# Plain products' results added by accumulating transfers, and dense matmuls dealt by engine time, in a transformer-layer kernel on one core

## The chip, the cores and the metric

The kernel runs on one core of a Trainium2 chip. Its engines are TensorE (PE: matmuls, with PEld for the loading of weights), VectorE (DVE), ScalarE (ACT), GpSimd (POOL) and SyncE (SP), which issues most of the transfers. Each engine works through its own queue in order; engines wait for one another by semaphores. Data lies in device memory (DRAM), in the on-chip memory (SBUF, 128 partitions) and in the matmul accumulators (PSUM).

The metric is the device time of one execution in microseconds (us); the median of several runs counts. A profiled execution also has a span, from its first to its last instruction.

## The reference

One layer, 2048 tokens, width 1024. The mixer has eight heads of stick-breaking attention (strictly causal) and eight heads of softmax attention over chunks with a relative bias; the MLP is a squared ReLU with 4096 hidden columns. Everything is float32.

```
mod = silu(c) @ w_ada + b_ada                 # shifts, scales and gates
h = rmsnorm(x, g_norm1) * (1 + sc1) + sh1
q_sb, k_sb, v_sb, q_ca, k_ca, v_ca = split(h @ w_in)
o_sb = stick_breaking_attention(q_sb, k_sb, v_sb)
o_ca = chunked_relpos_attention(rmsnorm(q_ca, g_q), rmsnorm(k_ca, g_k), v_ca, rel_bias)
x = x + gt1 * (concat(o_sb, o_ca) @ w_o)
h = rmsnorm(x, g_norm2) * (1 + sc2) + sh2
x = x + gt2 * (square(relu(h @ w1)) @ w2)     # the output
```

## The kernel before

All matmuls are done on pairs: a float32 operand is split by `split` (line 139) into a high part (a cast on ScalarE) and the remainder (a subtraction on VectorE), and `mm3` (line 206) multiplies them in three matmuls. The tokens stand in four blocks of 512 columns (`TB`); a block is `2 * mb + odd`, with `mb` the half of the sequence and `odd` the block in it. The residual stream lies in DRAM as `scr_x[block, row]`, eight rows of 128 channels; row `HK * r + n` is written as `r` (upper or lower half of the channels) and `n` (0 to 3).

**Projections** come first (to about 410 us), and then **attention** (to about 1277 us). Attention is a list of units: a head, a group `g` of 512 queries and, for stick-breaking, a block `c` of keys. Each unit takes four steps (`STEPS`), one for each 128 queries. The loop at line 1234 does for step i, in this order: the transposes of the weights of step i - 8 (`LAG`), the scan or softmax of step i (`soft1`: a sigmoid on ScalarE and a scan on VectorE into "p"), the split of the transposed weights ("wth", "wtl"), the matmuls with the values ("acc"), the scores of step i + 1 ("z", "cz", "ct"), and then `fill`. `fill` (line 1164) puts dense matmuls into TensorE's queue: the projections of the other two blocks ("pf") and the output projection ("po"), 1152 of them in all, taken from a list of generators. How many it takes follows from a credit: a share of the step is divided by the shares still to come and multiplied by the matmuls still to come. Before, the share is a constant of the unit: 0.7 for a stick-breaking unit on the diagonal, 1.0 off it, 0.9 for a softmax unit (0.68 in the last group), 0.6 in the eight closing steps. After each row block of results the dealing rests for a step, and for four at the start of some pieces; at changes between the kinds of units 4 or 8 matmuls are added.

**The MLP** (from line 1282) multiplies block matrices by a scheme of seven products in place of eight (Strassen's, in Winograd's form), and within most products once more: `First` makes the hidden rows, seven products per pair of row blocks, first for `mb` 1 and then for `mb` 0. Of the seven products of the second matrix, 1 and 6 are done plainly (`Second`, 16 steps of 12 matmuls) and the other five, `DOUBLE`, are themselves done in seven (`Outer`, 56 steps of 6 matmuls; the loop at line 1927). The products of both halves are joined in the doubled ones, and both halves have plain ones of their own. The steps form one list; `at(n, job)` hangs a job on step n, `later.add(k, job)` on the k-th tick from now, and `prepare` splits operands ahead of their step into a pool of eight tiles.

The plain products leave "s": product 1's result is needed by block (r 0, odd 1), and the sum of 1 and 6 by (0, 0), (1, 1) and (1, 0). `update` (line 1647) adds them to the residual stream, per half 16 times: SP loads the row from `scr_x` into a tile ("xu" in the second half's hidden products, two buffers lent by pool `rp`; else "txu", out of seven of pool `tp`), `weigh` (one VectorE instruction) adds "s" times the gate, and three ticks later SP stores the row. For `mb` 1 these updates stand in plain product 6 and in the following hidden products of `mb` 0 (four rows in each 16 steps); for `mb` 0 they stand in plain product 6, and in products 2, 3 and 4, where those of product 4 write the output.

Doubled product i loads the residual rows that it adds to (`load_x`, "txo" and "cxo"), adds its own results to them and stores them in `scr_x` or, where they are done, in the output. Products 7 and 5 serve two blocks each and have 16 such adds, the others 8. `half_sum` (line 1802) makes the sums of hidden rows ("r"), four VectorE instructions of 1024 columns for each kind; product 5 needs one kind more. `plan` places the loads and sums of the next product.

Of the kernel before, what the change touches and what calls it, by code (L numbers as in the profile page):

```python
# [79 lines left out]
def encoder_kernel(ctx, tc, xT, c, g1, g2, w_in, w_rest, gqk, bias, w_o, w1, w2, w_ada, b_ada, out):  # L80
# [5 lines left out]
    WIN, NEAR = 640, 384  # L86
    cpool = ctx.enter_context(tc.tile_pool(name="cpool", bufs=1))
# [90 lines left out]
    def norm_diagonal(pl, y, tg):  # L178
        dg = pl.tile([P, 4, P], F32, tag="ndg", name=f"ndg{tg}", bufs=1)
# [5 lines left out]
    def norm_rstd(pl, pp, acc, tg, meanwhile=None):  # L185
        y = norm_powers(pl, norm_columns(pp, acc, tg), tg)
        if meanwhile:
            meanwhile()
        return norm_diagonal(pl, y, tg)
# [488 lines left out]
    if True:  # L678
# [426 lines left out]
        def finish_row(g, n, ps, xr):  # L1105
# [28 lines left out]
            def spread(y):  # L1134
                dg = norm_diagonal(op, y, f"m{g}")
# [98 lines left out]
        for i in range(len(steps) + LAG):  # L1234
# [32 lines left out]
            fill(front.weight if front else 0.6, turns.get(i, 0))  # L1267
# [17 lines left out]
    DOUBLE = (7, 5, 2, 3, 4)  # L1285
# [10 lines left out]
    if True:  # L1296
# [43 lines left out]
        def norm2(tb, step):  # L1340
# [14 lines left out]
            def second():  # L1355
                dg = norm_rstd(np2, fresh, acc, f"m{tb}")
# [99 lines left out]
        class First(Step):  # L1456
# [29 lines left out]
            def fetch(self, m=None):  # L1486
                d = self.load()
                for n in range(4) if m is None else (m,):
# [3 lines left out]
                    elif pr == 5 and not self.mb:  # L1492
                        t = np2.tile([P, 4, P], F32, tag="ndg", name=f"s{self.nm}_{pr}", bufs=1).rearrange("p a b -> p (a b)")
# [227 lines left out]
        class Outer(Step):  # L1721
# [62 lines left out]
            def load_x(self, b):  # L1784
                home = kept if self.i in (5, 7) and b in ("22", "11") else temp
                for n in range(2):
                    Outer.outs[b, n] = []
                    for r, odd in {2: ((0, 1),), 3: ((0, 0),), 4: ((1, 1),), 7: ((1, 1), (1, 0)), 5: ((0, 0), (1, 0))}[self.i]:
# [3 lines left out]
                        Outer.outs[b, n].append((x, mb, row, odd, self.i in (2, 3, 4) or (self.i == 5 and mb and r)))  # L1792
# [81 lines left out]
        for mb in (1, 0):  # L1874
# [22 lines left out]
            if mb:  # L1897
# [29 lines left out]
        for i in DOUBLE:  # L1927
# [123 lines left out]
```

## Time and profile before

| | us |
|---|---|
| median of three runs | 2542.36 (2541.83 to 2547.02) |
| the profiled execution, whole | 2545.14 |
| the profiled execution, span | 2543.4 |
| granted TensorE clock, mean | 0.999 |

Columns of the views: a group of instructions has its line (a helper's, L42, for nearly all), engine, operation, "out<-in" by the names of the tiles, shape and count, then busy time in us, the mean of one in ns, the idle time of the engine before them and what ended it. Matmuls overlap: the next starts before the last has ended, and the ends are modelled, so that a short wait of TensorE doesn't show as idle. A row of a timeline has start, length, engine and tiles, with the idle time before it in brackets; SPq rows are transfers at their issue.

### The profile page before, as it was taken

The numbers are of one execution on the slowest core, as the hardware profiler recorded it, in microseconds if no ns is written. First come the engines' busy times: TensorE is split into PE (matmuls) and PEld (weight loads), VectorE is DVE, ScalarE is ACT, GpSimd is POOL, SyncE is SP. The second block draws the span as 40 slices with busy tenths as digits, with TensorE's granted clock in tenths as the row PEclk, the third lists the DMA queues.
The fourth block names the chain that finished last, engine by engine and source line by source line (L and its number), as shares of the span: only waits on it lengthen the run. The fifth ranks groups of instructions, "written<-read, shape, count | busy, mean of one in ns | idle before, by whom it ended". The sixth has DMA issues, their size and how long they took to land.

```text
span 2543.4 us, 39545 instructions
## 1 busy us (share of the span) xinstructions
PE 2513.3 (99%) x12388; PEld 2095.6 (82%) x12388; DVE 2053.9 (81%) x3609; ACT 1510.3 (59%) x2893; POOL 746.0 (29%) x1128
## 2 busy tenths in 40 slices
PE   9999999999999999999999999999999999999999
PEld 7888888888888888887988888888878888888887
DVE  7656767887789878999768777779877759899998
ACT  6333425668866677666755555566545546566665
POOL 4330154777776667776620000000000000000000
PEclk9999999999999999999999999999999999999999
DMA  9879969789977788866787889995998996868884
GB/s 362 323 296 365 351 267 301 208 243 287 290 234 237 236 250 274 265 212 206 218 310 254 302 279 318 329 362 195 328 331 283 313 365 261 329 241 308 282 300 124
DMA packets 305361, 714.66 MB, mean 281 GB/s; under 512 B 32768, under 2 KB 92160, under 8 KB 293504
## 3 DMA queue, kind: packets, MB, share of 16 engines
q1 hardware_dynamic: 303856, 707.43, 81.2%
q10 hardware_dynamic: 1296, 4.72, 0.5%
q8 instruction: 98, 1.61, 0.3%
q14 instruction: 111, 0.91, 0.1%
HBM read 485.00 MB, written 227.02 MB: 280 GB/s over the span
## 4 chain that ended last, share of the span: by engine, by line
PE 80%; DVE 10%; ACT 4%; issue 3%; DMA 3%; POOL 1%; SPq 0%; DVEq 0%; POOLq 0%; ACTq 0%
PE ps L42 24%; PE ps_s L42 14%; PE pt L42 11%; PE acc L42 6%; PE wt L42 6%; PE pf L42 4%; PE z L42 4%; PE po L42 4%; PE pq L42 3%; DVE opr L42 2%; DVE p L42 2%; PE cz L42 1%; DVE ol L42 1%; PE ct L42 1%; DVE r L42 1%
## 5 line engine op out<-in xcount | busy, mean ns | idle before, releaser
L42 PE MATMUL ps<-h,opw 128*128 128x512 f32 x1512 | 358.6, 389 | 0.0
L42 ACT CAST wth<-wt 128x512 fp32r<-128x512 f32 (+3 forms) x544 | 257.0, 483 | 166.7 <-PE wt L42 157.5
L42 POOL TENSOR_TENSOR b<-p 128x512 f32<-128x512 f32 (+1 forms) x320 | 292.0, 912 | 168.7 <-DVE p L42 93.8
L42 DVE TENSOR_TENSOR wtl<-wt,wth 128x512 fp32r<-128x512 f32 (+3 forms) x544 | 291.0, 546 | 57.6 <-ACT wth L42 55.6
L42 PEld LDWEIGHTS ps<-h,opw 128*128 128x128 f32 x1512 | 283.7, 188 | 58.9
L42 PE MATMUL pt<-w,ht 128*128 128x512 f32 x1248 | 288.2, 391 | 0.0
L42 PE MATMUL ps_s<-h,opw 128*128 128x512 f32 x1152 | 279.4, 392 | 4.0 <-DVE cp L42 3.4
L42 PEld LDWEIGHTS pt<-w,ht 128*128 128x128 f32 x1248 | 233.0, 188 | 47.7
L42 DVE TENSOR_TENSOR_SCAN p<-z,p,zero 128x512 f32<-128x512 f32 x192 | 245.7, 1281 | 25.6 <-ACT z L42 18.1
L42 PEld LDWEIGHTS ps_s<-h,opw 128*128 128x128 f32 x1152 | 216.8, 189 | 51.1 <-DVE cp L42 4.7
L42 ACT CAST opr<-r 128x512 fp32r<-128x512 f32 x280 | 174.4, 624 | 134.5 <-PE ps L42 75.9
L42 PE MATMUL ps<-opr,ol 128*128 128x512 f32 x960 | 222.2, 390 | 0.7 <-DVE opr L42 0.6
L42 PE MATMUL acc<-wth,v 128*128 128x512 f32 (+3 forms) x544 | 220.6, 410 | 0.0
L42 PEld LDWEIGHTS ps<-opr,ol 128*128 128x128 f32 x960 | 179.6, 188 | 40.9 <-DVE opr L42 3.5
L42 ACT ACTIVATE z<-z 128x512 f32<-128x512 f32 (+1 forms) x320 | 166.5, 521 | 55.4 <-PE z L42 49.4
L42 DVE TENSOR_TENSOR opr<-r,opr 128x512 fp32r<-128x512 f32 x280 | 184.9, 687 | 10.7 <-ACT opr L42 9.9
L42 PE MATMUL z<-k,q 128*128 128x512 f32 (+3 forms) x640 | 185.7, 372 | 7.7 <-DVE p L42 7.0
L42 PE MATMUL acc<-wtl,v 128*128 128x512 f32 (+3 forms) x544 | 185.4, 347 | 0.0
L42 PE MATMUL ps<-oph,opv 128*128 128x512 f32 x768 | 176.0, 390 | 0.8 <-DVE oph L42 0.3
L42 PE MATMUL wt<-ident,b 128*128 128x128 f32 x1088 | 171.3, 273 | 0.9 <-DVE p L42 0.6
L42 PEld LDWEIGHTS ps<-oph,opv 128*128 128x128 f32 x768 | 143.9, 188 | 32.4 <-DVE oph L42 1.2
L42 PEld LDWEIGHTS wt<-ident,b 128*128 128x128 f32 x1088 | 136.4, 140 | 41.4 <-DVE wtl L42 1.7
(219 smaller groups left out, 4904.0 us busy)
## 6 DMA issues: line engine op xcount, KB each, us to landing
r<-scr_hid SPq DMA_DIRECT2D x80, 512.0 KB, 6.5
q<-scr_q SPq DMA_DIRECT2D x128, 256.0 KB, 5.0
w<-in_w_dram SPq DMA_DIRECT2D x64, 512.0 KB, 5.9
k<-scr_k SPq DMA_DIRECT2D x240, 128.0 KB, 4.5
v<-scr_v SPq DMA_DIRECT2D x120, 256.0 KB, 4.0
wa<-in_w_ada_dram SPq DMA_DIRECT2D x48, 512.0 KB, 6.2
ow<-scr_wo SPq DMA_DIRECT2D x24, 1024.0 KB, 5.9
l<-scr_t SPq DMA_DIRECT2D x20, 1024.0 KB, 7.3
```

The source lines that it names most:

```text
L42: return lambda *x, **y: self.tc.keep_in_program_order(f(*x, **y))
```

## The change

1. **Dealing.** A new function, `step_shares`, gives each of the 456 steps a share of its own: an estimate of VectorE's time in the step, times a common factor, less an estimate of what TensorE has to do in it besides the dense matmuls; at least 0.15. The factor is chosen so that all of TensorE's work, dense matmuls at 0.227 us included, is spread as VectorE's is.
2. **Updates.** `update` with its load, VectorE add and store is gone. In its place ScalarE multiplies "s" by the gate (`scaled`), into a tile or in place, and GpSimd issues a transfer that adds the tile to the row in DRAM (`gather`, with `accum_op`). The block (0, 0) has a scaled tile of its own; (1, 1) and (1, 0) share one. All of `mb` 0's updates but those of plain product 6 now stand in product 2, twelve steps apart for each row block; those of `mb` 1 stand twelve steps apart in the hidden products.
3. **Order.** The doubled products go 7, 2, 5, 3, 4 in place of 7, 5, 2, 3, 4. Product 5 now writes the output for block (1, 0) of both halves. The sums of the products after 7 and after 2 have new places.
4. **Room.** A pool "padl" of 160 bytes a partition comes first and holds the small columns of the second norm; the diagonal matrices of the norms go into tiles that are there already ("otmp", "ndg"); the space for descriptors of GpSimd's transfers goes from 256 to 1024.

```diff
+        def step_shares(units, work):
+            def pace(n):
+                return 0.109 if n <= 2 * 128 - 20 else n * 0.000417 + 0.0135
+            def vec(n):
+                return n * 0.00105 + 0.08
+            def scores(u, qi):
+                if not u.ca:
+                    n = TB - (qi * P if u.diag else 0)
+                    return 2 * pace(n), n * 0.00227 + 0.1
+                n, hn = u.size(qi)
+                tail = n - hn
+                return 2 * pace(hn) + (4 * pace(tail) if tail and qi < 2 else 0), n * 0.0013 + 0.5
+            own, vector = [], []
+            total = STEPS * len(units)
+            for i in range(total + LAG):
+                t = v = 0.0
+                if i + 1 < total:
+                    t += scores(units[(i + 1) // STEPS], (i + 1) % STEPS)[0]
+                if i < total:
+                    v += scores(units[i // STEPS], i % STEPS)[1]
+                if i >= LAG:
+                    u, st = units[(i - LAG) // STEPS], (i - LAG) % STEPS
+                    nb = len(u.blocks)
+                    for kb, q0, q1 in u.blocks[nb * st // STEPS : nb * (st + 1) // STEPS]:
+                        t += (q1 - q0) * 0.109 + 2 * pace((q1 - q0) * P)
+                        v += vec((q1 - q0) * P)
+                own.append(t)
+                vector.append(v)
+            scale = (work * 0.227 + sum(own)) / sum(vector)
+            return [max(0.15, scale * v - t) for v, t in zip(vector, own)]
...
-        weight = STEPS * sum(u.weight for u in units) + LAG * 0.6
+        shares = step_shares(units, work)
+        weight = sum(shares)
...
-            fill(front.weight if front else 0.6, turns.get(i, 0))
+            fill(shares[i], turns.get(i, 0))
...
-    DOUBLE = (7, 5, 2, 3, 4)
+    DOUBLE = (7, 2, 5, 3, 4)
...
-        def update(mb, r, odd, loads, adds, home=None, last=False):
-            xs = {}
-            def fetch(n):
-                xs[n] = x = (home or temp)(f"xu{mb}_{r}{odd}_{n}")
-                sp.dma_start(x, scr_x[2 * mb + odd, HK * r + n])
-            def add(n):
-                x, row = xs[n], HK * r + n
-                weigh(x, Second.whole["s", n], row)
-                dst = rows_of(out, mb, row, odd) if last else scr_x[2 * mb + odd, row]
-                later.add(3, lambda: sp.dma_start(dst, x))
-            for n in range(HK):
-                at(loads[n], lambda n=n: fetch(n))
-                at(adds[n], lambda n=n: add(n))
+        def gather(mb, r, odd, n, x):
+            pool.dma_start(scr_x[2 * mb + odd, HK * r + n], x, accum_op=ALU.add)
+        def scaled(x, n, r):
+            row = HK * r + n
+            act.activation(x, Second.whole["s", n], AF.Identity, scale=mod[:, 5 * KT + row : 5 * KT + row + 1])
+            return x
+        def update(mb, n, step, home, last):
+            def one(r, odd):
+                x = scaled(home(f"xu{mb}_{r}{odd}_{n}"), n, r)
+                later.add(1, lambda: gather(mb, r, odd, n, x))
+            def two():
+                x = scaled(Second.whole["s", n], n, 1)
+                later.add(1, lambda: gather(mb, 1, 1, n, x))
+                at(step + 8, lambda: gather(mb, 1, 0, n, x))
+            if last:
+                at(step, lambda: one(0, 0))
+                at(step + 4, two)
+            else:
+                at(step, lambda: one(0, 1))
...
-                spread = lambda *ns: [f + n for n in ns]
-                update(mb, 0, 1, spread(0, 1, 2, 8), spread(4, 5, 6, 12))
+                for n, step in enumerate((4, 5, 6, 12)):
+                    update(mb, n, f + step, temp, False)
...
-                for n, (r, odd) in enumerate(((0, 0), (1, 1), (1, 0))):
-                    at_row = rest + 3 + 16 * n
-                    update(1, r, odd, range(at_row, at_row + 16, 4), range(at_row + 4, at_row + 20, 4), lent)
+                for n in range(HK):
+                    update(1, n, rest + 4 + 12 * n, lent, True)
...
-            spread = lambda *ns: [f + n for n in ns]
             if i == 2:
-                update(0, 0, 0, spread(8, 16, 24, 32), spread(14, 22, 30, 38))
-                pass
-            if i == 3:
-                update(0, 1, 1, spread(8, 16, 24, 32), spread(14, 22, 30, 38))
-            if i == 4:
-                update(0, 1, 0, spread(8, 16, 24, 32), spread(14, 22, 30, 38), None, True)
+                for n, step in zip((2, 3, 0, 1), range(f + 4, f + 52, 12)):
+                    update(0, n, step, temp, True)
             plan = {"load": {1: (f + 16, 4), 5: (f + 17, 2), 3: (f + 30, 2), 2: (f + 46, 2)}}
             plan["sum"] = {6: (e - 4, 4), 7: (e + 12, 4), 4: (e + 28, 4)}
+            if i == 2:
+                plan["sum"] = {5: (e - 14, 3), 6: (e - 2, 4), 7: (e + 13, 4), 4: (e + 28, 4)}
             if i == 7:
-                plan["sum"] = {5: (e + 1, 2), 6: (e + 8, 2), 7: (e + 28, 4), 4: (e + 44, 4)}
+                plan["sum"] = {6: (e + 8, 4), 7: (e + 28, 4), 4: (e + 44, 4)}
...
-    nc = _bacc.Bacc("TRN2", target_bir_lowering=False, num_devices=1, dynamic_dma_scratch_size=256)
+    nc = _bacc.Bacc("TRN2", target_bir_lowering=False, num_devices=1, dynamic_dma_scratch_size=1024)
```

More of the change, by code (lines that the diff above doesn't have):

```diff
@@ L86, in encoder_kernel @@
     WIN, NEAR = 640, 384
+    padl = ctx.enter_context(tc.tile_pool(name="padl", bufs=1))
+    padl.tile([P, 40], F32, tag="pad", name="padl")
     cpool = ctx.enter_context(tc.tile_pool(name="cpool", bufs=1))
@@ L176, in norm_powers, with norm_diagonal @@
         return y
-    def norm_diagonal(pl, y, tg):
-        dg = pl.tile([P, 4, P], F32, tag="ndg", name=f"ndg{tg}", bufs=1)
+    def norm_diagonal(pl, y, tg, home=None):
+        if home is None:
+            dg = pl.tile([P, 4, P], F32, tag="ndg", name=f"ndg{tg}", bufs=1)
+        else:
+            dg = home.rearrange("p (a b) -> p a b", b=P)
         dve.tensor_tensor(
@@ L183, in norm_diagonal, with norm_rstd @@
         return dg
-    def norm_rstd(pl, pp, acc, tg, meanwhile=None):
+    def norm_rstd(pl, pp, acc, tg, meanwhile=None, home=None):
         y = norm_powers(pl, norm_columns(pp, acc, tg), tg)
@@ L188, in norm_rstd @@
             meanwhile()
-        return norm_diagonal(pl, y, tg)
+        return norm_diagonal(pl, y, tg, home)
     def norm_spread(pp, dg, tg):
@@ L1134, in spread @@
             def spread(y):
-                dg = norm_diagonal(op, y, f"m{g}")
+                dg = norm_diagonal(op, y, f"m{g}", op.tile([P, TB], F32, tag="otmp", name=f"ndgm{g}"))
                 later.add(2, lambda: third(dg))
@@ L1355, in second @@
             def second():
-                dg = norm_rstd(np2, fresh, acc, f"m{tb}")
+                dg = norm_rstd(padl, fresh, acc, f"m{tb}", None, np2.tile([P, TB], F32, tag="ndg", name=f"ndgm{tb}", bufs=1))
                 def third():
@@ L1492, in fetch @@
                     elif pr == 5 and not self.mb:
-                        t = np2.tile([P, 4, P], F32, tag="ndg", name=f"s{self.nm}_{pr}", bufs=1).rearrange("p a b -> p (a b)")
+                        t = np2.tile([P, TB], F32, tag="ndg", name=f"s{self.nm}_{pr}", bufs=1)
                     else:
@@ L1791, in load_x @@
                         sp.dma_start(x, scr_x[2 * mb + odd, row])
-                        Outer.outs[b, n].append((x, mb, row, odd, self.i in (2, 3, 4) or (self.i == 5 and mb and r)))
+                        Outer.outs[b, n].append((x, mb, row, odd, self.i in (2, 3, 4) or (self.i == 5 and r > 0)))
         halves = {}
```

1 line of the change is left out of this document (added).

## The prediction

> **What bounds the kernel now.** I read the page first, then the windows by stage, then who waited for whom on TensorE, and last the chain of waits around the longest stall.
>
> ```profile
> span 2543.4 us, 39545 instructions
> PE 2513.3 (99%) x12388; PEld 2095.6 (82%) x12388; DVE 2053.9 (81%) x3609; ACT 1510.3 (59%) x2893; POOL 746.0 (29%) x1128
> ```
>
> TensorE is the bound and the change leaves its instructions as they are, so only its lost time can go: 2543.4 - 2513.3 = 30 us shown as idle, and what lies hidden under the modelled ends of its matmuls. The windows say where (columns: length, then busy time of PE, PEld, DVE, ACT, POOL). The first three are attention, by its groups of query blocks; the others are the plain product 6 of the first half, the second half's hidden products, the doubled products 5, 2, 3, and product 4 with the tail.
>
> ```profile
> 412.00:695.00 283.00, 275.48 (x1620) 235.06 (x1618) 228.77 (x546) 211.63 (x490) 204.14 (x295) 1.00 0.87 261
> 695.00:955.00 260.00, 256.58 (x1467) 216.49 (x1466) 224.20 (x441) 182.52 (x385) 173.48 (x252) 1.00 0.78 241
> 955.00:1277.00 322.00, 318.39 (x1830) 269.49 (x1828) 285.36 (x502) 219.58 (x439) 230.24 (x337) 1.00 0.74 235
> ...
> 1707.00:1750.60 43.60, 43.01 (x187) 34.50 (x185) 42.05 (x70) 31.60 (x56) 0.00 (x0) 1.00 0.67 241
> 1750.60:2056.00 305.40, 302.02 (x1322) 248.98 (x1323) 242.49 (x401) 160.03 (x285) 0.00 (x0) 0.99 0.89 300
> ...
> 2224.00:2300.00 76.00, 75.16 (x325) 60.27 (x324) 70.82 (x107) 47.03 (x81) 0.00 (x0) 1.00 0.70 249
> 2300.00:2376.00 76.00, 75.60 (x331) 61.67 (x330) 76.00 (x115) 49.26 (x85) 0.00 (x0) 1.00 0.85 303
> 2376.00:2452.00 76.00, 76.00 (x336) 62.76 (x335) 74.80 (x113) 50.23 (x86) 0.00 (x0) 1.00 0.83 290
> 2452.00:2543.40 91.40, 87.18 (x385) 71.69 (x383) 82.68 (x125) 54.00 (x92) 0.00 (x0) 0.99 0.54 175
> ```
>
> Idle TensorE is 7.5 us in attention's first third (283.00 - 275.48), 3.4 and 3.6 in the others, 0.6 in product 6, 3.4 in the hidden products, 0.8 and 0.4 in products 5 and 2, 0.0 in product 3; in the last window most is the tail after the last matmul. In attention TensorE waits for VectorE, and the hidden products have one long stall (idle time and releaser stand in brackets):
>
> ```profile
> PE z L42 <- DVE p L42: 7.0, 15, 1.2
> PE cz L42 <- DVE cols L42: 1.9, 4, 1.1
> ```
>
> ```profile
> 1883.76 2.88 PE L42 MATMUL ps<-h,opw 128*128 128x512 f32 x12
> 1889.56 4.57 PE L42 MATMUL ps_s<-h,opw 128*128 128x512 f32 x12 [2.92 <-DVE cp L42]
> ```
>
> It costs 2.92 us and then 4.57 - 2.88 = 1.69 us, since its 12 matmuls run slowly (granted clock 0.99 there, 1.00 in most other windows).
>
> **The change part by part.** First the dealing of attention's dense matmuls. Both versions deal 1152 of them over 456 steps and leave 96 for later. I worked the two rules through step by step, as arithmetic on the code: what a step has on TensorE besides, what VectorE has in it by the new rule's own formula, and how many dense matmuls each rule hands out at 0.227 us. That last agrees with the row above: 12 matmuls take 2.88 us with an overlapping end of 0.16, so 0.227 each from start to start. In steps 0 to 159 (the first window) the old rule deals 384, the new 408; in 160 to 287 it is 345 and 336, then 423 and 408. Summed over the steps in which VectorE has more to do than TensorE, the shortfall is 12.8 us in the first third and becomes 7.0; 7.2 becomes 6.9 and 12.9 becomes 12.0 in the others. So nearly all the gain lies in the first third. There TensorE's work is 179.0 + 384 x 0.227 = 266.2 us in a window of 283, so 16.8 us are lost, 7.5 of it visible. A cut by 5.8/12.8 = 45% is worth 3.4 us if only visible idle follows it and 7.6 if all does; I take 5.5, between them because waits shorter than the 0.16 us overlap are hidden but real. The rest loses 7.0 visible and falls by 1.2/20.1 = 6%: 0.4, or 1 with what is hidden. Attention: -6.5 us. The other end is a loss: the new rule has 60 steps without a dense matmul instead of 33, so +3 us (half its visible idle in the first third again).
>
> Second, the plain results. Of 32 updates each has today an SP load, a VectorE add and an SP store.
>
> ```profile
> L42 DVE SCALAR_TENSOR_TENSOR txu<-cs,mod,txu 128x512 f32<-128x512 f32 x20 | 14.9, 746 | 0.0
> L42 DVE SCALAR_TENSOR_TENSOR xu<-cs,mod,xu 128x512 f32<-128x512 f32 x12 | 8.9, 745 | 0.0
> ```
>
> ```profile
> xu<-scr_x SPq DMA_DIRECT2D x12, 256.0 KB, 4.4
> scr_x<-xu SPq DMA_DIRECT2D x12, 256.0 KB, 7.1
> ```
>
> ```profile
> L42 ACT ACTIVATE cy<-cy,mod,aff 128x512 f32<-128x512 f32 x20 | 14.7, 805 | 4.1 <-DVE cy L42 4.1
> ```
>
> VectorE loses 14.9 + 8.9 = 23.8 us. ScalarE gets 24 scalings (three per row block, the third tile serves two transfers); the nearest row is 0.805, so 19 us, 6.4 of them in the hidden products and 6.4 in product 2, where it is busy 160 of 305 and 49 of 76: hidden, and without that cover at most 0.8 each ahead of an operand's cast. GpSimd issues 32 accumulating transfers; it is at 0.00 busy in all these windows, nothing is queued behind them there. No row shows such a transfer: it lasts between 4.4 us (one load) and 11.5 (load and store after each other, 4.4 + 7.1); I take 8. Its first reader is a load on SP, behind which all later loads stand. The shortest way is from the last row of plain product 6 (second half) to product 2's first residual: 3 steps of 12 matmuls and 9 of 6, (36 + 54) x 0.227 = 20.4 us. Row for row it is hidden.
>
> What it frees is seen at the long stall. The chain of waits (start, us, what) and the queues' timeline:
>
> ```profile
> 1873.65 0.40 ACT cz L42
> 1874.04 4.86 DMA to<-scr_hid
> ...
> 1880.86 0.61 issue
> ...
> 1889.56 4.57 PE ps_s L42 x12
> ```
>
> ```profile
> 1869.05 0.37 SPq L42 DMA_DIRECT2D scr_t<-wt  x1
> ...
> 1873.19 0.32 SPq L42 DMA_DIRECT2D xu<-scr_x  x1
> 1873.57 0.90 SPq L42 DMA_DIRECT2D to<-scr_hid  x2
> ...
> 1880.81 0.75 DVE L42 SCALAR_TENSOR_TENSOR xu<-cs,mod,xu 128x512 f32<-128x512 f32 x1
> ```
>
> ```profile
> SPq L42 <- DMA scr_x<-xu: 24.8, 11, 4.8
> ```
>
> SP stood still until 1873.19, waiting for an update's store to land before it reloaded that buffer; such waits are 24.8 us here. The "to" loads behind it landed late (4.86 us after 1874.04), VectorE then worked without a pause to 1889.5, one update (0.61 on the chain) among it. Without the update the loads go up to 3.7 us sooner (SP's transfer before ended at 1869.4) but may wait for a buffer or ScalarE's cz, which ends at 1874.05: gain 0.61 to 4.6 us; I take 2 of the idle and 1 of the slow stretch, -3. What is late next is the same VectorE, by under 1 us. In product 6 of the first half VectorE is busy 42.05 of 43.60 and loses four adds, 3.0 us: between 0 and -1.5 (0.6 idle, the rest hidden); -1. Product 3 has no idle to give back, product 4 little: 0.
>
> The Trainium skill ("DMA: Bandwidth & Descriptors", section "Issuing engines are not separate DMA queues") says that transfers from another engine's queue share the same 16 DMA engines and save only issue time. By that rule this part gives about 0 and the sum is 4 us higher; the row of 24.8 us of waits speaks for more, as the wait belongs to SP's place in line.
>
> Third, order 7, 2, 5. Product 2 now follows plain product 6, and product 5, with 16 residual adds, follows product 2. VectorE per 8 steps of 10.9 us:
>
> ```profile
> 2296.44 0.69 DVE L42 TENSOR_TENSOR ol<-l,ol 128x512 fp32r<-128x512 f32 x1
> 2297.05 1.30 DVE L42 TENSOR_TENSOR opr<-r,opr 128x512 fp32r<-128x512 f32 x2
> 2298.25 0.69 DVE L42 TENSOR_TENSOR ol<-l,ol 128x512 fp32r<-128x512 f32 x1
> 2298.85 0.69 DVE L42 TENSOR_TENSOR opr<-r,opr 128x512 fp32r<-128x512 f32 x1
> 2299.45 2.73 DVE L42 SCALAR_TENSOR_TENSOR cxo<-ps,mod,cxo 128x512 f32<-128x512 f32 x4
> ...
> 2306.91 1.23 DVE L42 TENSOR_TENSOR r<-r,r 128x1024 f32<-128x1024 f32 x1
> 2308.04 1.30 DVE L42 TENSOR_TENSOR opr<-r,opr 128x512 fp32r<-128x512 f32 x2
> ```
>
> Three operand halves take 2298.25 - 2296.44 = 1.81, so 7.2 per 8 steps; two sums 2.3 (2308.04 - 2306.91 = 1.13 each), four adds 2.7: 12.2, so product 5 runs 1.3 short per 8 steps from step 12 to 40 in either order, on operands prepared ahead. In the new order product 2's last 14 steps carry four more sums, about 11.6 per 8 steps, 1.2 in debt, and product 5's first 12 steps give 1.8 back. Between +4.6 (3.5 groups, nothing prepared) and -1.2 (the idle of both windows); I take 0. The moved tiles (the diagonal in "otmp" and "padl", the larger descriptor space) add no instruction: 0.
>
> **Sum.** -6.5 - 3 - 1 = -10.5 us against the profiled execution's 2545.14 (span 2543.4 and 1.7 around it): 2534.6. It ran 2.8 over the median of the runs, 2542.36; with that off, 2532.
>
> **The rivals.**
> A, attention's waits do not follow the shares (they are the latency of single scans, 0.47 us on average, 7.0/15, not a lack of work): +6.5, 2538.5. For it: the longest of the 15 is 1.2 us, half a step. Against: half the idle lies in the first third, where the old rule deals least for what VectorE has.
> B, the first third loses nothing any more: 16.8 instead of 5.5, 2521. For it: the new shares fit the scans step by step. Against: 7.0 us of shortfall remain.
> C, product 5 falls behind: +4.6, 2537. For it: VectorE at 76.00 of 76. Against: its 12 light steps.
> D, slower: uneven dealing. In 82 steps the new rule deals two or more above the old one; they put a lump of TensorE work between one score and the next, the scan behind it starts late, and VectorE, busy 81 to 89% in attention's windows, does not catch up. At one matmul, 0.227, per such step it costs 18.6 instead of gaining 6.5: 2532 + 25 = 2557. It decides from 18 such steps on, where the 4 us of the other part are used up, and can be measured from 40. Against: scores are issued before the dense matmuls of their step.
> E, the transfers come late. If GpSimd gets to its descriptors only when VectorE pauses, the twelve of product 2 begin at its end: 12 x 1.04 (the row below) + 11.5 = 24 us, where 15 are left to product 5's residual; SP loses 9 and with 4 covered by prepared operands the kernel 5: 2537.
>
> ```profile
> L42 POOL TENSOR_TENSOR b<-p 128x512 f32<-128x512 f32 x224 | 233.1, 1041 | 156.0 <-DVE p L42 90.3 <-PE wt L42 17.7 <-PE z L42 16.3
> ```
>
> The Trainium skill ("SBUF — State Buffer", section "Who interferes with whom") says that GpSimd shares a port pair with VectorE, so that descriptors made by GpSimd can be held up. The row shows GpSimd working beside a VectorE that is 81 to 89% busy; no run here shows descriptors.
>
> **How the numbers follow.** Forecast 0.50 (alone 2528 to 2538: attention -3.4 to -8.6 and the rest -0.6 to -6.1 from 2542.4), A 0.15, B 0.11, C 0.07, D 0.12, E 0.05. A measurement of this kernel tells 0.2% (5 us) from no change, so faster is below 2537.3: 0.47 of the forecast, B, half of C and E, 0.64; same 0.24; slower D, 0.12. The range starts at B and ends at 2546, where attention takes its other end, +3, and the rest brings nothing; it leaves out D and part of B.
>
> **What would show it.** Right: TensorE's idle in the first third falls from 7.5 to about 4; the stall at 1889 shrinks below 1 us; no SP wait for an update's store is left; GpSimd shows 32 issues and nothing waits for them. Wrong: SP waiting for an accumulating transfer, more TensorE waits for "p" than 15, or product 5 with more than 2 us idle.

## The result and the profile after

| | before | after |
|---|---|---|
| median of seven runs each, us | 2544.05 (2541.83 to 2547.02) | 2536.95 (2535.44 to 2538.57) |
| ratio after to before, 95% interval | | 0.9968 (0.9958 to 0.9977) |
| the profiled execution, whole / span, us | 2545.14 / 2543.4 | 2536.57 / 2534.8 |

The change makes the kernel faster by 0.32%: 8.1 us by the ratio, 7.1 by the medians. First the page after:

```profile
span 2534.8 us, 39551 instructions
PE 2511.2 (99%) x12388; PEld 2097.2 (83%) x12388; DVE 2032.4 (80%) x3577; ACT 1523.8 (60%) x2917; POOL 773.9 (31%) x1160
```

VectorE has 32 instructions fewer, ScalarE 24 more, GpSimd 32 more: the parts that the diff names. TensorE's own work is unchanged, 12388 matmuls. The windows of the same stages follow (attention's thirds, moved by a microsecond as the stages moved; then the hidden products, which belong to `mb` 0):

```profile
413.00:696.00 283.00, 278.64 (x1630) 237.57 (x1629) 227.96 (x541) 210.51 (x486) 202.60 (x294) 1.00 0.87 266
696.00:956.00 260.00, 255.50 (x1471) 216.13 (x1470) 224.08 (x445) 183.72 (x390) 176.91 (x255) 1.00 0.79 244
956.00:1276.00 320.00, 316.39 (x1819) 267.82 (x1818) 284.91 (x501) 218.93 (x440) 228.88 (x335) 1.00 0.73 229
```

```profile
1750.60:2056.00 305.40, 305.13 (x1346) 252.45 (x1345) 235.15 (x390) 168.03 (x297) 11.12 (x13) 1.00 0.91 299
```

Length less TensorE's busy time is 4.4, 4.5 and 3.6 us in attention's thirds (before 7.5, 3.4 and 3.6): the first third gave 3.1 back, the second took 1.1. In the hidden products 0.3 is left of 3.4 us, and GpSimd's 11.12 us there are the issues of the new transfers. Who ends TensorE's waits, in attention (a row is: who waits for whom, us in all, times, longest):

```profile
PE z L42 <- DVE p L42: 5.5, 11, 1.0
PE cz L42 <- DVE cols L42: 1.4, 2, 1.0
```

and after 1700 us, in the hidden products (one row, where before there were 3.4 us, 2.9 of them in one wait):

```profile
PE ps_s L42 <- DVE cp L42: 0.3, 1, 0.3
```

So the long stall at 1889 is gone. One row speaks against the forecast, the only one of its kind. SP waits once for an accumulating transfer:

```profile
SPq L42 <- DMA scr_x<-txu: 6.3, 1, 6.3
```

It is the last row of plain product 6: GpSimd issues it at 2213.57 us, it lands at 2220.53, and SP stands from 2214.24 until then before product 2's first residual. TensorE loses nothing by it (70.00 of 70 us busy from 2220 to 2290).

What the page can't show is the time hidden under the modelled ends of matmuls. I therefore counted it from the trace as well: from the start of each matmul to the start of the next, less the pace that `step_shares` has for that width (0.227 us for 512 columns). This is a count of mine and no view of the profile:

| lost by TensorE, start to start, us | before | after |
|---|---|---|
| attention, steps 0 to 159 | 18.0 | 14.2 |
| attention, steps 160 to 287 | 12.3 | 12.7 |
| attention, steps 288 on | 12.3 | 12.4 |
| first half's plain product 6 | 1.5 | 0.4 |
| the stall at 1889 | 4.7 | 0 |
| products 2 and 5, loss at operands | 3.7 | 3.5 |

The last row moved as a whole: before, it stood about product 5 in its old place (2269 to 2371 us), after, at 2337 to 2363 us, where product 5 now stands.

One figure of the description ahead of the prediction has to be corrected. Products 7 and 5 have 24 residual adds each and products 2, 3 and 4 have 12 each (84 rows "txo" and "cxo" in all), not 16 and 8. The prediction's working by groups of four adds per 8 steps doesn't depend on it, but products 7 and 5 have half as many adds again as that sentence says.

### The profile page after: what moved, and what is told of

It is laid out like the page before. It is cut to its first block, busy times and chain, and to the rows that moved or that the text cites. A ratio compares the mean times of both kernels' runs of the same rounds, so it can differ in the third digit from the quotient of the medians.

```text
span 2534.8 us, 39551 instructions
## 1 busy us (share of the span) xinstructions
PE 2511.2 (99%) x12388; PEld 2097.2 (83%) x12388; DVE 2032.4 (80%) x3577; ACT 1523.8 (60%) x2917; POOL 773.9 (31%) x1160
## 4 chain that ended last, share of the span: by engine, by line
PE 48%; DVE 7%; ACT 1%; DMA 1%; issue 1%; SPq 0%; POOL 0%; DVEq 0%; ACTq 0%; POOLq 0%
PE ps L42 25%; PE ps_s L42 14%; PE po L42 3%; PE acc L42 2%; PE wt L42 2%; DVE opr L42 2%; PE z L42 1%; DVE ol L42 1%; DVE r L42 1%; DVE h L42 1%; DVE txo L42 0%; PE cz L42 0%; ACT cy L42 0%; DVE cy L42 0%; ACT h L42 0%
## 5 line engine op out<-in xcount | busy, mean ns | idle before, releaser
L42 DVE TENSOR_TENSOR_SCAN p<-z,p,zero 128x512 f32<-128x512 f32 x192 | 245.5, 1280 | 21.2 <-ACT z L42 16.4
L42 DVE TENSOR_TENSOR opr<-r,opr 128x512 fp32r<-128x512 f32 x280 | 184.4, 681 | 10.8 <-ACT opr L42 10.0
L42 POOL DMA_DIRECT2D scr_x<-txu x12 | 10.5, 878 | 546.8 <-ACT txu L42 546.8
```

The source lines that it names most:

```text
L42: return lambda *x, **y: self.tc.keep_in_program_order(f(*x, **y))
```

## The experiments

All ratios are to the kernel before, run on the same chip in turn with the experiment. The order below is that of the questions, not of the runs.

### The two halves of the change apart

The dealing alone, put into the kernel before (the function `step_shares` comes with it):

```diff
...
-        weight = STEPS * sum(u.weight for u in units) + LAG * 0.6
+        shares = step_shares(units, work)
+        weight = sum(shares)
...
-            fill(front.weight if front else 0.6, turns.get(i, 0))
+            fill(shares[i], turns.get(i, 0))
```

> The kernel before with the new shares alone. Theory (the parts add up: dealing -3, second half's transfers -5 to -6, the rest 0): 2541 against 2544, with TensorE's idle in 412 to 695 us near 4.4 instead of 7.5 and the stall at about 1889 us unchanged (2.9 us). Rival A (dealing moves stalls, removes none): 2544, TensorE idle over the whole of attention unchanged at 14.6.

And the change without it, the same edit backwards:

> The changed kernel with the old constant shares. Theory: 2539 (2544 - 5), the stall in the second hidden products gone, attention's TensorE idle 14.6 as before. Rival A: 2537, all of the gain is here.

The first gives 2540.58 us, ratio 0.9989 (0.9980 to 0.9998); the second 2540.86, ratio 0.9983 (0.9975 to 0.9992); before had 2544.65 there. In microseconds that is -2.8 (-0.5 to -5.1) for the dealing and -4.3 (-2.0 to -6.4) for transfers and order, together -7.1 of the change's -8.1: within these intervals the halves add up. The forecast had -6.5 and -4. So the MLP's part was right in size and attention's more than twice too large. The profiled execution of the first was a long one (2549.81, with 3.3 us of waits for transfers in attention), so no attention window is read from it. In its place stands the count from start to start over the other kept traces: attention's first third loses 18.0 to 19.7 us in the five with the old shares and 14.0 to 16.6 in the seven with the new ones, the variants below included. The first has the stall of before in the hidden products, the second nothing like it:

```profile
PE ps_s L42 <- DVE cp L42: 4.2, 2, 4.0
```

```profile
PE ps_s L42 <- DVE cp L42: 0.3, 1, 0.3
```

### Where the transfers help

The kernel before, with transfers for the updates of `mb` 1 alone (its plain product 6 and the hidden products that follow), the order and the updates of `mb` 0 as they were (`update_t` is the change's `update`; the room of the change's fourth point comes with it):

```diff
-                update(mb, 0, 1, spread(0, 1, 2, 8), spread(4, 5, 6, 12))
+                if mb:
+                    for n, step in enumerate((4, 5, 6, 12)):
+                        update_t(mb, n, f + step, temp, False)
+                else:
+                    update(mb, 0, 1, spread(0, 1, 2, 8), spread(4, 5, 6, 12))
...
-                for n, (r, odd) in enumerate(((0, 0), (1, 1), (1, 0))):
-                    at_row = rest + 3 + 16 * n
-                    update(1, r, odd, range(at_row, at_row + 16, 4), range(at_row + 4, at_row + 20, 4), lent)
+                for n in range(HK):
+                    update_t(1, n, rest + 4 + 12 * n, lent, True)
...
```

> The kernel before with accumulating transfers for the half mb 1 alone (plain product 6 and the hidden products); order 7, 5, 2 and the updates of mb 0 as before. Theory: 2539, as with all transfers, since the moved order and the first half's transfers bring nothing. Rival (order and first half bring 2 to 3 of it): 2541 to 2542.

2540.13 us, 0.9983 (0.9974 to 0.9992): the same as with both halves' transfers and the new order (2540.86). Half the transfers bring the whole gain; those of `mb` 0, and the order 7, 2, 5, bring nothing that shows. By the count from start to start product 5 loses 3.7 us, as before.

### What made the stall at 1889: VectorE's add or SP's place in line

The prediction gave the gain there two causes, the add on VectorE (0.61 us on the chain) and the transfers on SP behind a buffer that was not free. Two kernels part them. In the first, the twelve updates of the hidden products keep a VectorE instruction of the same size and lose the load and the store:

```diff
             def fetch(n):
                 xs[n] = x = (home or temp)(f"xu{mb}_{r}{odd}_{n}")
-                sp.dma_start(x, scr_x[2 * mb + odd, HK * r + n])
+                if not home:
+                    sp.dma_start(x, scr_x[2 * mb + odd, HK * r + n])
...
+                if home:
+                    s = Second.whole["s", n]
+                    dve.scalar_tensor_tensor(x, s, mod[:, 5 * KT + row : 5 * KT + row + 1], s, op0=ALU.mult, op1=ALU.add)
+                    return
```

> The kernel before; the 12 updates in the second hidden products keep VectorE's add (of other data) and leave out SP's load and store. Theory (SP's wait): the stall at about 1889 us goes to under 1 us, 2540. Rival (VectorE's load): it stays near 2.9 us, 2544.

In the second they keep load and store and lose the add:

```diff
-                weigh(x, Second.whole["s", n], row)
+                if not home:
+                    weigh(x, Second.whole["s", n], row)
```

> The kernel before; the same 12 updates keep SP's load and store and leave out VectorE's add. Theory (SP's wait): the stall stays at 2 to 3 us, 2543 to 2544. Rival (VectorE's load): it falls under 1 us, 2540.

Neither kernel adds the plain results to the residual stream in these twelve places. Without load and store: 2541.05 us against 2545.6, ratio 0.9982 (0.9973 to 0.9991). Without the add: 2544.39, 0.9994 (0.9985 to 1.0004). The intervals overlap, so it is the traces that part the two. The window of the hidden products, of the first and then of the second:

```profile
1750.60:2056.00 305.40, 304.74 (x1342) 251.15 (x1341) 245.52 (x407) 162.03 (x288) 0.00 (x0) 1.00 0.84 283
```

```profile
1750.60:2056.00 305.40, 301.03 (x1317) 247.71 (x1316) 237.19 (x393) 159.95 (x284) 0.00 (x0) 0.99 0.88 300
```

Read the third busy time, VectorE's. With the add and without SP's transfers it is 245.52 us, more than the 242.49 of before, and TensorE idles 0.7 us. Without the add it is 237.19, and TensorE idles 4.4. The profiled execution of the second was its longest (2549.97), but its timeline shows the same stall, 5 us later and again released by VectorE's "cp":

```profile
1887.98 2.88 PE L42 MATMUL ps<-h,opw 128*128 128x512 f32 x12
1894.76 4.57 PE L42 MATMUL ps_s<-h,opw 128*128 128x512 f32 x12 [3.90 <-DVE cp L42]
```

All kept traces say the same: the stall (2.9 to 4.0 us) is there in the three kernels that keep these loads and stores (before, the dealing alone, this one) and in none of the ten others. So it is SP's side that makes it: a load that waits for its buffer's store holds up the loads behind it, and VectorE is late because its data is. Less traffic is not the reason: the change moves as much in this window (299 GB/s, before 300, the last column), and the "to" loads take no less time from issue to landing, before and then after:

```profile
to<-scr_hid SPq DMA_DIRECT2D x31, 256.0 KB, 5.7
to<-scr_hid SPq DMA_DIRECT2D x32, 256.0 KB, 6.4
```

They start sooner: the first of the four at the place 16.0 us ahead of the stalled matmuls before, and 20.4 and 21.2 us ahead of the same matmuls without load and store and in the change. Whether SP's standing still (24.8 us of waits before) or the 24 issues themselves weigh more, these two kernels don't part; the medians of an issue are 0.32 us for a load and 0.56 for a store, so all 24 take about half as long as the waits.

### ScalarE or VectorE for the scalings

The change, with `scaled` as a VectorE instruction:

```diff
-            act.activation(x, Second.whole["s", n], AF.Identity, scale=mod[:, 5 * KT + row : 5 * KT + row + 1])
+            dve.scalar_tensor_tensor(
+                x, Second.whole["s", n], mod[:, 5 * KT + row : 5 * KT + row + 1], zero.to_broadcast([P, TB]),
+                op0=ALU.mult, op1=ALU.add,
+            )
```

> The changed kernel with its 24 scalings on VectorE (0.75 us each, in place of ScalarE's 0.72), the transfers as changed. It puts 18 of the 23.8 us back on VectorE and leaves SP free. If the stall at 1889 us came from SP's wait for the lent buffer: 2537, no stall over 1 us in the second hidden products. If it came from VectorE's load: 2540, the stall is back with 1 to 3 us.

2544.01 us, 0.9993 (0.9984 to 1.0002): neither of the two times expected. Nearly all of the change's gain is gone, though the stall at 1889 stays away. By the count from start to start it goes in small pieces, in plain product 6 (1736 to 1749 us), at 1771 and 1810, and about products 2 and 5; the largest wait in the hidden products is now this one:

```profile
PE ps_s L42 <- DVE cp L42: 1.8, 2, 1.4
```

VectorE's load doesn't make the stall at 1889, but 24 instructions of 0.75 us on it are paid for in other places, some 6 us of 18 (3 to 10 by the two intervals). That they went to ScalarE is as much a part of the gain as the transfers.

### Attention: the pause, the least share, the later thirds

Three edits of the dealing. The pause after a row block of results, on top of the change:

```diff
-        RESTS = {"wait": 4, "start": 0}
+        RESTS = {"wait": 2, "start": 0}
```

> The changed kernel with a pause of 2 steps instead of 4 where a piece of dense work begins. In the changed kernel 61 steps of attention have no dense matmul and lose about 14 us against the pace of the matmuls, 3.3 and 3.1 us in two of the pauses. If the pause costs this: 2532 (-5). If the pause covers the loads of the piece's operands, TensorE waits for these transfers instead: 2537 or more, with waits <- DMA fx.

2537.18 us, 0.9971 (0.9961 to 0.9982), the same as the change itself (0.9968), and without the waits for "fx" that the second answer wanted. By my count the thirds lose 14.9, 10.8 and 13.7 us: the waits moved from the second third to the third, and 1.5 us of waiting for the output projection's weights came up at 1302 us. By the prediction's arithmetic this dealing has 7.6, 6.2 and 9.6 us of shortfall, 2.5 less than the change's 7.0, 6.9 and 12.0, and none of it came back.

The other two stand on top of the last kernel of these experiments (products 7 and 5 with transfers too, below), whose dealing is the change's. A larger least share, so that fewer steps are without dense matmuls:

```diff
-            return [max(0.15, scale * v - t) for v, t in zip(vector, own)]
+            return [max(0.3, scale * v - t) for v, t in zip(vector, own)]
```

> The kernel of the run before (products 7 and 5 with transfers too), with one figure of the dealing changed: the least share of a step is 0.3 in place of 0.15. By the same arithmetic on the code, VectorE's shortfall in attention's thirds stays at 7.6, 6.7 and 11.5 us (7.0, 6.9, 12.0 with 0.15), but the steps without a dense matmul fall from 60 to 32. Theory (what attention still loses, it loses in steps without dense matmuls): visible idle in the second and third window falls from 4.5 and 3.6 to about 4.0 and 3.0, and the time by 1 to 2.5 us, to about 2532. Rival (what is left belongs to the shortfall or to single scans, wherever the matmuls stand): the same idle within 0.3 in each window, 2533.6.

The new shares in the first third alone:

```diff
         shares = step_shares(units, work)
+        old = [u.weight for u in units for _ in range(STEPS)] + [0.6] * LAG
+        back = sum(shares[160:]) / sum(old[160:])
+        shares[160:] = [back * w for w in old[160:]]
```

> The same kernel with 0.15 again, the new shares in steps 0 to 159 alone and the old constants, scaled to the same sum, in the others. By the arithmetic the shortfall is 7.0, 10.0 and 14.7 us in the thirds (7.0, 6.9, 12.0 with the new shares throughout) and the steps without a dense matmul 45 in place of 60. If the shortfall sets the lost time, as the prediction has it, the second and third window's idle rises by some 2 us together, 2535.5. If the steps without dense matmuls set it, their idle falls back to the 3.4 and 3.6 of before, 2532.5. In either case the first window keeps its 4.4.

The least share of 0.3: 2533.28 us, 0.9949 (0.9936 to 0.9963), nothing beside the 0.9954 of the kernel that it stands on. The first third alone: 2538.22, 0.9969 (0.9956 to 0.9981), 3.8 us worse than that kernel by the ratios, 4.9 worse than the least share of 0.3 by the medians on the same chip. Attention's windows, of the kernel that both stand on, then with 0.3, then with the old constants after the first third:

```profile
413.00:696.00 283.00, 277.88 (x1625) 236.36 (x1624) 226.91 (x538) 209.51 (x484) 201.89 (x293) 1.00 0.87 265
696.00:956.00 260.00, 255.45 (x1469) 215.99 (x1468) 224.53 (x446) 183.95 (x391) 177.17 (x255) 1.00 0.80 244
956.00:1276.00 320.00, 316.37 (x1821) 267.47 (x1820) 284.26 (x502) 218.98 (x439) 229.27 (x335) 1.00 0.74 230
```

```profile
413.00:696.00 283.00, 278.21 (x1628) 237.35 (x1627) 227.22 (x540) 209.49 (x485) 202.20 (x294) 1.00 0.88 265
696.00:956.00 260.00, 254.95 (x1470) 215.27 (x1469) 224.65 (x448) 183.72 (x390) 177.51 (x254) 1.00 0.78 245
956.00:1276.00 320.00, 316.59 (x1825) 267.92 (x1824) 285.19 (x504) 221.65 (x443) 230.94 (x337) 1.00 0.73 231
```

```profile
413.00:696.00 283.00, 278.61 (x1633) 237.49 (x1632) 228.54 (x544) 210.55 (x488) 203.28 (x295) 1.00 0.86 267
696.00:956.00 260.00, 254.11 (x1466) 215.03 (x1465) 223.61 (x442) 183.45 (x388) 176.16 (x253) 1.00 0.77 241
956.00:1276.00 320.00, 315.19 (x1800) 266.07 (x1800) 283.49 (x493) 217.72 (x433) 227.21 (x334) 0.99 0.72 229
```

Idle TensorE is 5.1, 4.6 and 3.6 us in the first, 4.8, 5.0 and 3.4 in the second: 13.3 and 13.2 in sum. So the steps without dense matmuls are not where the rest is lost. (The first third of the first has the same dealing as the change and 5.1 where that had 4.4: one window differs by some 0.7 from one execution to another.) In the third kernel the first third keeps its 4.4, and the others rise to 5.9 and 4.8, 2.5 us together, as the shortfall had it (2); the time rose by 3.8, twice the 1.9 expected. A part of that is one stretch at half the granted clock, the third figure from the end of this row:

```profile
1198.50:1201.80 3.30, 3.30 (x14) 2.99 (x13) 3.30 (x5) 1.19 (x3) 2.73 (x4) 0.50 0.76 202
```

So the shortfall tells which dealing is worse where it differs by 5.8 us; the 2.5 us of the shorter pause did not show.

### Is product 5 short of VectorE?

First a way to take work off VectorE that failed. Eight of product 5's sums of hidden rows on GpSimd:

```diff
-            column_sum(dve, t, halves[x, g], halves[y, g], ALU.subtract)
+            column_sum(pool if i == 5 and pr in (7, 4) else dve, t, halves[x, g], halves[y, g], ALU.subtract)
```

> The changed kernel with eight of product 5's sums of hidden rows (the kinds for its fifth and seventh inner product) on GpSimd, which does nothing else there. If VectorE's load bounds product 5: its 3.5 us of lost time at 2336 to 2363 us go, 2534. If GpSimd's sums are late or slow VectorE's subtractions down: 2537 or more, with waits <- POOL r.

2547.29 us, 1.0009 (1.0000 to 1.0018): some 10 us lost against the change. Groups at the place, in this kernel and then in the change (busy us, mean ns, then idle before):

```profile
L42 DVE TENSOR_TENSOR opr<-r,opr 128x512 fp32r<-128x512 f32 x18 | 23.5, 1337 | 0.0
...
L42 POOL TENSOR_TENSOR r<-r,r 128x1024 f32<-128x1024 f32 x8 | 22.0, 2765 | 26.8 <-DVE r L42 22.6 <-PE ps L42 4.2
```

```profile
L42 DVE TENSOR_TENSOR opr<-r,opr 128x512 fp32r<-128x512 f32 x30 | 19.7, 678 | 0.0
```

An "opr" takes 1337 ns in the mean instead of 678, and the timelines of GpSimd and VectorE show why:

```profile
2308.30 2.72 POOL L42 TENSOR_TENSOR r<-r,r 128x1024 f32<-128x1024 f32 x1 [4.23 <-DVE r L42]
```

```profile
2308.70 2.88 DVE L42 TENSOR_TENSOR opr<-r,opr 128x512 fp32r<-128x512 f32 x1
```

VectorE's instruction begins while GpSimd's runs and ends after it: it stands for as long as GpSimd works. Not all of the 10 us is this. TensorE's waits are followed by a stretch at half the granted clock, in which 15 matmuls take 6.8 us instead of 3.4:

```profile
2329.60:2339.70 10.10, 6.80 (x15) 4.62 (x15) 10.10 (x8) 2.29 (x4) 6.41 (x3) 0.50 0.31 116
```

The run says nothing on product 5's need, as it took VectorE's time instead of giving it.

Then the change's own means. Products 7 and 5 treat the blocks that they don't finish as the plain results: ScalarE scales their first part out of the accumulators, GpSimd issues accumulating transfers, and one tile serves both blocks of product 7:

```diff
-                        weigh(x, ps, row)
-                        if done:
-                            dst = rows_of(out, mb, row, odd) if last else scr_x[2 * mb + odd, row]
-                            later.add(2, lambda dst=dst, x=x: sp.dma_start(dst, x))
+                        if x is None:
+                            home = kept if b == "22" else temp
+                            x = e[0] = home(f"xo{self.i}_{b}_{n}{odds[0]}")
+                            act.activation(x, ps, AF.Identity, scale=mod[:, 5 * KT + row : 5 * KT + row + 1])
+                        else:
+                            weigh(x, ps, row)
+                        if done and last:
+                            later.add(2, lambda dst=rows_of(out, mb, row, odds[0]), x=x: sp.dma_start(dst, x))
+                        elif done:
+                            for odd in odds:
+                                later.add(2, lambda dst=scr_x[2 * mb + odd, row], x=x: pool.dma_start(dst, x, accum_op=ALU.add))
...
```

> The changed kernel, with the change's own means taken further: doubled products 7 and 5 treat the blocks that they do not finish as the plain products' results now are. ScalarE scales their first part out of the accumulators, VectorE adds the second part where there is one, and GpSimd issues accumulating transfers; where two blocks of product 7 take the same rows, one tile serves both. VectorE loses 20 of product 7's 24 adds and 8 of product 5's 24 (0.68 us each, so 13.6 and 5.4 us), and SP loses 24 loads and 24 stores. My theory (in product 5 VectorE is short, and the 3.5 us lost start to start there come back with its load): 5.4 us are more than the 3.5 lost, and product 7 has some 0.4 to give, so 2533, 3.5 below the changed kernel, ratio to before 0.9955. Rival 1 (the loss in product 5 is due to the latency of single operands, not to VectorE's load): unchanged, 2537. Rival 2 (ScalarE's scalings stand ahead of the casts of operands, and TensorE waits for these): 2539 or more, with waits of TensorE that ScalarE ends in products 7 and 5.

2533.6 us, 0.9954 (0.9941 to 0.9968): 3.4 us under the change by the medians, as forecast, and the fastest of these kernels together with the one with the least share of 0.3. VectorE's residual adds fall from 84 to 56; TensorE's waits after 1890 us are

```profile
PE ps L42 <- DVE opr L42: 0.3, 1, 0.3
PE ps_s L42 <- DVE cp L42: 0.2, 1, 0.2
```

and none is ended by ScalarE. By the count from start to start, product 5 loses 0.9 us instead of 3.5. The run takes work off SP's queue too, but in the changed kernel VectorE (third busy time) has no idle time at the place, so it wasn't waiting for loads:

```profile
2269.00:2345.00 76.00, 75.98 (x334) 62.41 (x333) 76.00 (x112) 50.99 (x88) 3.32 (x4) 1.00 0.86 287
2345.00:2421.00 76.00, 74.84 (x323) 60.01 (x322) 76.00 (x115) 48.62 (x83) 0.00 (x0) 1.00 0.88 304
```

So that loss was VectorE's load.

## Why the prediction was right, and where its sizes were not

**The time.** 2532 was forecast and 2536.95 measured, in the range; but the range, 2521 to 2546, held the time before as well, so that being in it says little. Of the 5 us between them 3.7 are attention's (-6.5 forecast, -2.8 by the dealing alone), 1.7 the starting point and -0.3 the rest (-4 forecast, -4.3 measured; the count from start to start gives -5.8, inside the interval). The starting point: I took 2.8 us off because the profiled execution ran over the median of three, 2542.36; the median of seven is 2544.05, and the later ones, of 9 to 33 runs, lie from 2543.56 to 2545.6. Three runs from 2541.83 to 2547.02 didn't bear that correction.

**Attention, -6.5: right in kind, mis-sized.** The first third's idle fell from 7.5 to 4.4, "about 4" as announced. The step that failed is "a cut by 45% is worth 3.4 us if only visible idle follows it and 7.6 if all does": it scaled all 16.8 us of lost time by the relative fall of the shortfall. What came back is a part of the shortfall's own difference. In the first third it fell by 5.8 us and the loss by 3.8 from start to start. In the later thirds, from the old constants scaled to the new ones, it falls by 5.8 (24.7 to 18.9) and the loss by 4.2 (29.3 to 25.1), of which 1.5 belong to the stretch at half clock. That is 0.5 to 0.7 us per us, and the sum of 5.8 + 1.2 would be worth 3 to 5 us instead of 6.5; the dealing alone measured 2.8 (0.5 to 5.1). The forecast of -0.4 to -1 for the later thirds was not met (24.6 became 25.1 us), and neither a shorter pause nor fewer steps without dense matmuls got the rest back. What sets it stays open; single scans are a candidate ("p" still ends 11 waits of 0.5 us), not tried alone.

**The stall at 1889, -3: right in mechanism, taken too small.** It gave back 4.7 us, at the upper end of the 0.61 to 4.6 that I had bounded it by. I took 2 of the idle, as the "to" loads might wait for a buffer or for "cz" instead; the whole stall went. SP's side carried it and not the add (0.61): the two kernels that part them show it. The Trainium skill ("DMA: Bandwidth & Descriptors", section "Issuing engines are not separate DMA queues") says that issuing from several engines saves only the issue time; this part would then have been about 0. No run moves a load and store as they are to another queue, so that sentence is not tried alone here. What the runs add is that 24 transfers fewer on SP are worth 4.5 us (0.9982, with VectorE's work kept), as a transfer that must wait holds up those behind it in the same queue.

**Plain product 6, -1:** 1.5 us of loss became 0.4. **The order, 0:** right; its loss of 3.5 us moved with product 5. **ScalarE's cover:** the scalings take 0.72 us (estimate 0.805), and no wait of TensorE is ended by them. Costing them at nothing was right; the same work on VectorE costs some 6 us.

**The transfers.** GpSimd's issues and, from issue to landing, the medians:

```profile
L42 POOL DMA_DIRECT2D scr_x<-cs x16: 844/880/1202, 1777.4 to 2284.9; - x16
L42 POOL DMA_DIRECT2D scr_x<-txu x12: 844/857/1083, 1725.9 to 2278.9; - x12
L42 POOL DMA_DIRECT2D scr_x<-xu x4: 847/861/870, 1765.5 to 1864.1; - x4
```

```profile
scr_x<-cs POOLq DMA_DIRECT2D x16, 256.0 KB, 8.1
scr_x<-txu POOLq DMA_DIRECT2D x12, 256.0 KB, 7.0
scr_x<-xu POOLq DMA_DIRECT2D x4, 256.0 KB, 7.9
```

32 issues, as announced, and 7.0 to 8.1 us where I took 8 between 4.4 and 11.5. In the rows of SP's waits from 1704 to 1910 us there is no wait for an update's store or for an accumulating transfer any more; the largest for a transfer is now

```profile
SPq L42 <- DMA scr_t<-wt: 8.1, 8, 2.5
```

At 2214 us there is one, the 6.3 us shown above. It was named ahead as a sign of being wrong, and it is: the prediction put 20.4 us of TensorE's steps between that transfer and its first reader, but SP's queue was ahead of those steps and reached the load 0.7 us after the issue. The step "row for row it is hidden" failed there, and that it cost nothing is luck as far as the runs show.

**The rivals.** E (transfers late) fell: in product 2's stretch VectorE is busy 67.81 of 70 us and GpSimd's twelve issues still take 0.87 each, 10.39 in all:

```profile
2220.00:2290.00 70.00, 70.00 (x310) 58.02 (x309) 67.81 (x101) 50.01 (x87) 10.39 (x12) 1.00 0.86 260
```

D (slower by lumps) fell: the waits for "p" went from 15 to 11 and from 7.0 to 5.5 us. C didn't come about, as product 5 lost 3.5 us where it had lost 3.7, but its ground was right: VectorE is short there. B fell with the 4.4 us that stay. A's time, 2538.5, is nearer than the forecast's, and C's and E's, 2537, are nearer still, but a near time doesn't make the mechanism: A's (the waits don't follow the shares at all) is refuted by the first third, and by the later thirds with the old constants, where the idle time rose with the shortfall.

## What to carry to other kernels

A stall whose releaser is a busy engine may come from a queue two steps behind it: test the engine's work and the queue's transfers apart before moving either. A store and reload of a lent buffer on the one queue that feeds everything can cost more than its issue time; an accumulating transfer from an idle engine takes both away. It pays where that queue or VectorE is what others wait for (here -4.3, then -3.4 us) and not elsewhere: the transfers for `mb` 0 brought nothing. Shares dealt by an engine's shortfall are worth a part of the shortfall's own difference, here 0.5 to 0.7 of 5.8 us, and not a share of all the time that is lost; differences of 1 to 3 us didn't show.

## What the runs showed of the hardware

A GpSimd addition of two operands in on-chip memory (2.72 to 2.82 us for 128 x 1024) stops a VectorE instruction that reads two such operands for as long as it runs (0.68 us became 2.88 in the row shown), while GpSimd's issues of accumulating transfers beside a VectorE at 97% are not lengthened beyond 1.2 us. The Trainium skill ("SBUF — State Buffer", section "Who interferes with whom") has both: the blocking between two instructions that read in this way, and, as an inference, that this kind of VectorE instruction does not hold up GpSimd's descriptors; the rows agree with both.

A long stall of TensorE has a second price: a stretch of 3.4 us, or a multiple, at half the granted clock (0.50, the third figure from the end). Kernel before, load and store without the add, and the dealing alone, after 2.9, 3.9 and 4.0 us of idle time:

```profile
1889.60:1892.80 3.20, 3.20 (x8) 2.55 (x9) 2.94 (x5) 2.09 (x4) 0.00 (x0) 0.50 1.10 342
1896.00:1899.20 3.20, 3.20 (x9) 2.43 (x9) 1.36 (x3) 0.93 (x2) 0.00 (x0) 0.50 1.08 342
1892.60:1899.20 6.60, 5.82 (x14) 4.57 (x15) 3.97 (x7) 3.21 (x7) 0.00 (x0) 0.50 1.06 379
```

In the first two the next 12 matmuls take 4.57 us instead of 2.88, 1.69 more; in the third the stretch is twice as long and they take 5.49. After 0.46 us of idle time (before, 1987 us) they take 3.06, and the clock is 1.00. So the second price is not read off the length of the stall alone.
